# Two-layer hybrid decoder trunk in fp32: output tiles from both PSUM pools, one more pair by seven products, softmax division on either engine

## The chip, the cores and the metric

The kernel runs on one core of a Trainium2 chip. The metric is the device time of one execution in microseconds (us); the kernel before has a median of 2092.57 us over three runs (2092.12 to 2093.74). Engines are named as in the profile: PE (TensorE, matmul), DVE (VectorE), ACT (ScalarE), POOL (GpSimd), SP (SyncE, which issues the loads).

## The reference, cut to what matters

x is 512 tokens by 1024, c one row of 1024, everything fp32. Each of two layers does three sub-layers, each with a shift, a scale and a gate computed from c (adaLN). D_FF is 2816.

```python
for each layer:
    (shift, scale, gate) x 3 = SiLU(c) @ w_mod + b_mod
    x += 1/2 * gate1 * FFN1(RMSNorm(x) * scale1 + shift1)      # SwiGLU
    x += gate2 * (concat[A, B, C](RMSNorm(x) * scale2 + shift2, w_in) @ w_out)
    x += 1/2 * gate3 * FFN2(RMSNorm(x) * scale3 + shift3)
FFN(h) = (silu(h @ w_gate) * (h @ w_up)) @ w_down
A = stick-breaking attention (4 heads), B = dilated attention (4 heads, softmax over three
window patterns), C = HGRN2 gated linear recurrence (4 heads)
```

## The kernel before

**Numbers.** Activations lie transposed: 128 rows of the model dimension by 512 tokens, eight such tiles for x (`X[d]`). A product in fp32 is made of three matmuls on operands split into a high and a low part (`triple`). A weight tile is loaded as `w` (128x1024), cast to a high part by ACT (`wt<-w`) and subtracted to a low part by DVE (`wt<-w,wt`).

**Phases.** Net 0 (FFN1 of layer 0, to about 393 us), mixer 0 (to 698), net 1 (FFN2, to 1063), net 2 (FFN1 of layer 1, to 1418), mixer 1 (to 1723), net 3 (FFN2, to the end). `MOD` holds the adaLN columns; `background()` computes them for later sub-layers beside the nets: DVE accumulates rows of w_mod times c in `acc`, reduces `acc` to `p`, PE multiplies `p` by `quads` in one small matmul, and DVE writes four pieces of `mod`.

**One net (`ffn`).** The 22 hidden blocks of 128 go in three groups of 8, 8 and 6. In a group PE first makes the hidden blocks in pairs, gate then up, and then the eight output tiles of 128x512 (`x += gate * sum over the group's blocks`). A pair is dense (48 matmuls of 512 columns into pool `m` for the gate, 48 into pool `a` for the up) or, if its first block f is in `FAST[net]`, made by a scheme of seven products (`seven`, `empty`, `combine`): 84 matmuls of 256 columns for the gate and 84 for the up, with more sums of weights and partial results on DVE and ACT.

**PSUM.** Eight banks of 128x512 lie in two pools: `M` has two (named m in the profile), `B` has six (named a). A dense gate and, before, every output tile of a net take m banks; a gate by seven products takes two m and one a; an up takes two or three a. The small adaLN matmul and the sum of squares of the norm take an a bank.

**Output tiles.** The first two of a group are made by `down_two`, both at once, in two pieces (all blocks but the last two, then those). The others are made one by one by `down`. In the last group of nets 0 to 2 the last six are made in two halves of 256 columns. After each, `residual` on DVE adds the tile to x (`x<-m,mod,x`), which needs that sub-layer's `mod` and frees the bank.

**The head of a phase.** `first()` makes the first pair of the next phase for half of the tokens at a time; it asks for two m banks, then two a banks.

**What sets the order.** The program is static. At build time `Flow.run` keeps a list of streams, each at a `Step` on some engine, with estimated clocks of the engines (`F.clk`, `Flow.cost`) and estimated ready times of the tiles. It emits the step whose estimated start plus a bias is smallest, if the pools it needs have room. Every instruction is issued through `Engine.call`, so the profile has line L116 for nearly all. For a PE step of the background stream (rank 4) `Flow.start` adds `LATE` to the ready times of what it reads, so that it is put later in PE's order.

**Mixers.** Projections, and for each head tasks that run in four lanes beside them. `dilated` makes the softmax of the dilated heads: scores on PE, mask and maximum on DVE, exponential with its sum on ACT, reciprocal of the sum and division on DVE.

Of the kernel before, what the change touches and what calls it, by code (L numbers as in the profile page):

```python
# [14 lines left out]
AF = mybir.ActivationFunctionType  # L15
ALU = mybir.AluOpType
# [28 lines left out]


GROUPS = (8, 8, 6)
FAST = ((4, 8, 12, 16, 18), (4, 8, 10, 12, 14, 16, 18), (4, 8, 10, 12, 14, 16, 18), (4, 8, 10, 12, 14, 16, 18, 20))


PROJ = "f0,q0,g0,i0,qa,ka,va,q1,f1,g1,qb,i1,kb,vb"
# [11 lines left out]
BR = -0.15  # L63
BA = (-0.1, -0.1)
BN = (-0.15, -0.1)
LATE = 2.0
LOP = ((1, 2, 3), (1, 2, 3, 4, 5, 6, 7))

SPANS = tuple((sum(GROUPS[:i]), n) for i, n in enumerate(GROUPS))
# [159 lines left out]
class Flow:  # L229
# [96 lines left out]
    def start(self, s):  # L326
# [6 lines left out]
        t = self.clk[st.engine] if st.engine != "SP" else self.clk["PE"]  # L333
        late = self.MARGIN if st.engine == "PE" and s[0] == 0 else LATE if st.engine == "PE" and s[0] == 4 else 0.0
        for a in st.deps:
# [24 lines left out]
def trunk(ctx, tc, x, c, w_mod, b_mod, f1g, f1u, f1d, w_in, w_out, qng, kng, hng, lbl, f2g, f2u, f2d, cf, out):  # L360
    nc = tc.nc
    F = Flow()
    V, A, G, T, Q, Q2 = (Engine(F, e, n) for e, n in (
        (nc.vector, "DVE"), (nc.scalar, "ACT"), (nc.gpsimd, "POOL"), (nc.tensor, "PE"), (nc.sync, "SP"),
        (nc.gpsimd, "SP")))

    def space(name, bufs, **kw):
        return ctx.enter_context(tc.tile_pool(name=name, bufs=bufs, **kw))
# [8 lines left out]
    M = Pool(F, space("psm", 2, space=PS), "m", [P, S], 2)  # L377
    B = Pool(F, space("psa", 6, space=PS), "a", [P, S], 6)

    def small(w=1):  # L380
        return col.tile([P, 8], F32, tag="c", name="c")[:, :w]
# [33 lines left out]
    def when(*keys):  # L415
        return lambda: all(k in done for k in keys)
# [339 lines left out]
    def plan():  # L756
# [6 lines left out]
        for l in range(DEPTH):  # L763
            for wg, wu, wd, last in ((f1g, f1u, f1d, 0), (f2g, f2u, f2d, 1)):
                net = 2 * l + last
                its = []
                for f0, n in SPANS:
                    for f in range(f0, f0 + n, 2):
                        kind = "f" if f in FAST[net] else "w"
                        its += [(kind, [(0, w[l, :, f * P:(f + 2) * P], ND, 256)]) for w in (wg, wu)]  # L770
# [172 lines left out]
    def part(w, k, i=None):  # L943

        o = slice(0, 256) if i is None else slice(i * P, (i + 1) * P)
        return tuple(z[:, k % 4, o] for z in w[k // 4])

    def triple(ps, wh, wl, xh, xl, start, stop, skip=False):
        T.matmul(ps, wh, xh, start=start, stop=False, skip_group_check=skip)
        T.matmul(ps, wh, xl, start=False, stop=False, skip_group_check=skip)  # L950
        T.matmul(ps, wl, xh, start=False, stop=stop, skip_group_check=skip)
# [164 lines left out]
    def start_norm(phase, l, jsh, orders=(tuple(range(ND)),) * 2, after=None):  # L1116
        hs = [None] * ND
        hold.append(phase)
        quads4 = None if jsh == 3 or not FAST[2 * l + (jsh > 0)] else [[None] * 4 for _ in range(4)]
        for t in range(2):  # L1120
# [15 lines left out]
    def residual(phase, d, ps, l, jg, cs):  # L1136
        if jg != 5 or not isinstance(phase, tuple):
            yield when(("mod", l, jg))
        yield Step("DVE", ps, bias=BR)
        V.scalar_tensor_tensor(X[d][:, cs], ps[:, cs], mod(l, jg, d), X[d][:, cs], ALU.mult, ALU.add)  # L1140
        drop(ps)
        for t in range(2):
            if cs.start <= t * HALF and cs.stop >= (t + 1) * HALF:
                done.add((phase, d, t))
# [32 lines left out]
    def ffn(phase, l, jsh, hs, last):  # L1177
        jg = jsh + 2
        nhs = None
        fast = FAST[2 * l + (jsh > 0)]  # L1180
        for f0, n in SPANS:
# [58 lines left out]
            for f in range(f0, f0 + n, 2):  # L1240
# [15 lines left out]
                if f in fast:  # L1256
                    yield when((phase, "sums"))
                    for name, pools, fin in (("g", (M, M, B), gate_seven), ("u", (B, B, B), up_seven)):
                        w = yield from next_weight()
                        yield Step("PE", need=tuple((p, pools.count(p)) for p in (M, B) if p in pools))  # L1260
                        banks = [p.get() for p in pools]
# [6 lines left out]
                for pool, fin in ((M, gate_out), (B, up_out)):  # L1268
                    w = yield from next_weight()
                    for i in range(2):  # L1270
                        yield Step("PE", need=((pool, 1),))
                        ps = pool.get()
# [17 lines left out]

            def down(w, d, cs):
                yield when(keys[0])
                yield Step("PE", need=((M, 1),))
                ps = M.get()
                for k in range(n):
                    yield when(keys[k])
                    hi, lo = hid[k]
                    wh, wl = part(w, k, d % 2)
                    yield Step("PE", lo, wh, wl)
                    triple(ps[:, cs], wh, wl, hi[:, cs], lo[:, cs], k == 0, k == n - 1)  # L1300
                F.spawn(residual(key, d, ps, l, jg, cs), 0)

            def down_two(w, cuts):

                yield Step("PE", need=((M, 2),))
                banks = [M.get() for _ in range(2)]
                for ks in cuts:
                    for d, ps in enumerate(banks):
                        for k in ks:
                            yield when(keys[k])  # L1310
                            hi, lo = hid[k]
                            wh, wl = part(w, k, d)
                            yield Step("PE", lo, wh, wl)
                            triple(ps, wh, wl, hi, lo, k == 0, k == n - 1)
                        if ks[-1] == n - 1:
                            F.spawn(residual(key, d, ps, l, jg, FULL), 0)
# [4 lines left out]
            for d in range(0, whole, 2):  # L1321
                w = yield from next_weight()
                if d == 0:
                    yield from down_two(w, (range(n - 2), range(n - 2, n)))
                else:
                    for i in range(2):
                        yield from down(w, d + i, FULL)
                release(w)
# [32 lines left out]
    def mixer(phase, l, hs):  # L1361
# [4 lines left out]
        def key(*k):  # L1366
            return (phase, *k)
# [327 lines left out]
        def drop_qk(name, hp):  # L1695
            got["qk", name, hp] = got.get(("qk", name, hp), 0) + 1
            if got["qk", name, hp] == 2:
                U.put(*got["q" + name, hp], *got["k" + name, hp])
# [105 lines left out]
        def dilated(h):  # L1804
            hp, r = h // 2, 64 * (h % 2)
            yield when(key("qb", hp), key("kb", hp), *(key("vb", t) for t in range(NT)))
            qh, ql = got["qb", hp]
            kt = got["kb", hp][h % 2]
            kh, kl = kt[:, :S], kt[:, S:]
            yield Step("PE", ql, kt, need=((U, 9),))  # L1810
            sm = [U.get() for _ in range(3)]
            part = {3: sm[0], 2: sm[1][:, :384], 0: sm[1][:, 384:], 1: sm[2][:, :256]}
            for i in (3, 2, 1, 0):
                n = (i + 1) * P
                qc = slice(i * P, n)
                yield Step("PE", need=((B, 1),))
                s = B.get()
                T.matmul(s[:, :n], qh[:, qc], kh[:, :n], start=True, stop=False)
                T.matmul(s[:, :n], qh[:, qc], kl[:, :n], start=False, stop=False)
                T.matmul(s[:, :n], ql[:, qc], kh[:, :n], start=False, stop=True)  # L1820
                mx, den = small(), small()
                yield Step("DVE", s)
                V.tensor_tensor_reduce(part[i], s[:, :n], C["dil"][:, S - n:], 1.0, NEG, ALU.add, ALU.max, accum_out=mx)
                B.put(s)
                V.tensor_scalar(mx, mx, -1.0, None, ALU.mult)
                yield Step("ACT", mx)
                A.activation(part[i], part[i], AF.Exp, bias=mx, accum_out=den)
                yield Step("DVE", den)
                V.reciprocal(den, den)
                V.tensor_scalar(part[i], part[i], den, None, ALU.mult)  # L1830
            drop_qk("b", hp)
            wh, wl = [None] * 3, [None] * 3
            for b, cs in ((1, (1, 3)), (2, (2,)), (0, (0,))):
                n = WIDTH[b]
                yield Step("PE", *sm, need=((B, 1),))
                pt = B.get()
                for c_ in cs:
                    o = SEG[c_][1]
                    for i in range(c_, NT):
                        T.transpose(pt[:, o + (i - c_) * P:o + (i - c_ + 1) * P], part[i][:, c_ * P:(c_ + 1) * P], ident)  # L1840
                yield Step("ACT", pt, need=((U, 2),))
                wh[b], wl[b] = U.get(F32R), U.get(F32R)
                A.copy(wh[b][:, :n], pt[:, :n])
                yield Step("DVE", wh[b])
                V.tensor_sub(wl[b][:, :n], pt[:, :n], wh[b][:, :n])
                B.put(pt)
            U.put(*sm)
            yield from attend("b", "vb", h, wh, wl)
# [56 lines left out]
        for d in range(0, ND - 2, 2):  # L1905
            w = yield from next_weight()
            yield Step("PE", need=((M, 2),))
            banks = [M.get() for _ in range(2)]
# [10 lines left out]
        for t, cs in enumerate(HALVES):  # L1919
            for n, d in enumerate(order[t]):  # L1920
                pool = (M, B)[n % 2]
                yield Step("PE", need=((pool, 1),))
                ps = pool.get()
# [65 lines left out]
```

## Time and profile before

| | |
|---|---|
| median of three runs | 2092.57 us |
| the profiled execution | 2094.81 us, span 2092.4 us |
| mean granted TensorE clock | 0.992 |
| matmuls of 512 columns into m, into a | 3444, 800 |
| matmuls of 256 columns into m, into a | 3684, 3718 |
| weights and constants read | 255 MB, 123 GB/s over the span |

The costliest groups of instructions (engine, operation, tiles, forms, count, then busy us and mean ns of one, then idle time before them and its most frequent releaser):

```profile
L116 ACT CAST wt<-w 128x1024 fp32r<-128x1024 f32 (+1 forms) x456 | 437.6, 975 | 328.4 <-PE m L116 124.0
L116 DVE TENSOR_TENSOR wt<-w,wt 128x1024 fp32r<-128x1024 f32 (+1 forms) x456 | 518.6, 1144 | 95.3 <-ACT wt L116 86.2
L116 PE MATMUL m<-u,wt 128*128 128x512 f32 (+1 forms) x2820 | 576.7, 362 | 6.3 <-DVE x L116 4.2
L116 PE MATMUL m<-h,wt 128*128 128x256 f32 (+1 forms) x2892 | 551.8, 342 | 11.6 <-ACT h L116 5.5
```

A time in a group is the sum over its instructions; matmuls overlap one another, so the mean of one is longer than the distance from one to the next. A name such as m<-u,wt says that a tile of pool m was written from u and wt: m<-u,wt in a net is an output tile, m<-h,wt or a<-h,wt a dense gate or up, a<-hs,wt and m<-hs,wt belong to the seven products, and a<-p,quads is the small matmul of the adaLN columns. Rows of the timeline give the start, the length, the engine, the operation and its count; in brackets stands the idle time of the engine ahead of it and what ended it.

### The profile page before, as it was taken

The numbers are of one execution on the slowest core, as the hardware profiler recorded it, in microseconds if no ns is written. First come the engines' busy times: TensorE is split into PE (matmuls) and PEld (weight loads), VectorE is DVE, ScalarE is ACT, GpSimd is POOL, SyncE is SP. The second block draws the span as 40 slices with busy tenths as digits, with TensorE's granted clock in tenths as the row PEclk, the third lists the DMA queues.
The fourth block names the chain that finished last, engine by engine and source line by source line (L and its number), as shares of the span: only waits on it lengthen the run. The fifth ranks groups of instructions, "written<-read, shape, count | busy, mean of one in ns | idle before, by whom it ended". The sixth has DMA issues, their size and how long they took to land.

```text
span 2092.4 us, 32600 instructions
## 1 busy us (share of the span) xinstructions
PE 2050.3 (98%) x12956; PEld 1855.7 (89%) x12956; DVE 1586.0 (76%) x2510; ACT 1005.1 (48%) x1675; POOL 183.6 (9%) x224
## 2 busy tenths in 40 slices
PE   7999999999999999999999999999999999999999
PEld 6888889988888987999898899989888889889897
DVE  6887877686698776879686888867867978658584
ACT  5523434555855542544354253436476645325351
POOL 0000000150150100000010000012304200000000
PEclk8999999999999999999999999999999999999999
DMA  9376466211203245345524635643112141533321
GB/s 330 117 230 191 151 218 204 81 60 41 71 21 99 94 133 169 109 154 182 181 69 134 221 101 181 197 146 102 41 41 66 36 127 55 186 96 101 101 82 41
DMA packets 210569, 259.46 MB, mean 124 GB/s; under 512 B 8896, under 2 KB 192084, under 8 KB 210416
## 3 DMA queue, kind: packets, MB, share of 16 engines
q1 hardware_dynamic: 210160, 257.30, 38.5%
q8 instruction: 101, 1.65, 0.3%
q14 instruction: 52, 0.43, 0.1%
q0 software_dynamic: 256, 0.08, 0.0%
HBM read 255.25 MB, written 2.10 MB: 123 GB/s over the span
## 4 chain that ended last, share of the span: by engine, by line
PE 93%; DVE 4%; ACT 2%; issue 1%; DMA 1%; SPq 0%; DVEq 0%; ACTq 0%
PE m L116 56%; PE a L116 37%; ACT u L116 1%; DVE u L116 1%; DVE wt L116 1%; DVE x L116 1%; DVE h L116 1%; DVE acc L116 0%; ACT wt L116 0%; DMA w<-in_ffn_w_up_dram 0%; DMA u<-in_x_dram 0%; DVE k L116 0%; ACT L1471 0%; ACT L116 0%; SPq L116 0%
## 5 line engine op out<-in xcount | busy, mean ns | idle before, releaser
L116 ACT CAST wt<-w 128x1024 fp32r<-128x1024 f32 (+1 forms) x456 | 437.6, 975 | 328.4 <-PE m L116 124.0
L116 DVE TENSOR_TENSOR wt<-w,wt 128x1024 fp32r<-128x1024 f32 (+1 forms) x456 | 518.6, 1144 | 95.3 <-ACT wt L116 86.2
L116 PE MATMUL m<-u,wt 128*128 128x512 f32 (+1 forms) x2820 | 576.7, 362 | 6.3 <-DVE x L116 4.2
L116 PE MATMUL m<-h,wt 128*128 128x256 f32 (+1 forms) x2892 | 551.8, 342 | 11.6 <-ACT h L116 5.5
L116 PEld LDWEIGHTS m<-u,wt 128*128 128x128 f32 x2820 | 475.4, 190 | 85.7 <-DVE x L116 5.6
L116 PEld LDWEIGHTS m<-h,wt 128*128 128x128 f32 x2892 | 451.0, 192 | 69.4 <-ACT u L116 6.6
L116 PE MATMUL a<-h,wt 128*128 128x256 f32 (+1 forms) x2124 | 347.4, 318 | 0.0
L116 PEld LDWEIGHTS a<-h,wt 128*128 128x128 f32 x2124 | 308.3, 191 | 26.5
L116 DVE TENSOR_TENSOR u<-u 128x256 f32<-128x256 f32 (+4 forms) x444 | 255.3, 593 | 34.5 <-ACT u L116 30.7
L116 PE MATMUL a<-hs,wt 128*128 128x256 f32 x1944 | 250.8, 283 | 0.0
L116 POOL TENSOR_TENSOR u<-u 128x256 f32<-128x256 f32 x162 | 137.6, 869 | 1284.8 <-ACT u L116 1237.5
L116 PEld LDWEIGHTS a<-hs,wt 128*128 128x128 f32 x1944 | 241.0, 192 | 0.0
L116 DVE SCALAR_TENSOR_TENSOR x<-m,mod,x 128x512 f32<-128x512 f32 (+1 forms) x142 | 92.2, 651 | 111.7 <-PE m L116 111.0
L116 ACT ACTIVATE u<-u 128x512 f32<-128x512 f32 (+2 forms) x272 | 146.7, 567 | 49.2 <-POOL u L116 29.3
L116 DVE TENSOR_TENSOR w<-w 128x512 f32<-128x512 f32 x216 | 149.0, 690 | 6.2 <-DMA w<-in_ffn_w_gate_dram 0.6
L116 DVE SCALAR_TENSOR_TENSOR acc<-w,sc_c,acc 128x1024 f32<-128x1024 f32 x112 | 143.6, 1282 | 1.8
L116 PEld LDWEIGHTS a<-u 128*128 128x128 f32 x864 | 114.7, 191 | 11.8 <-issue 2.1
L116 ACT COPY u<-a 128x256 f32<-128x256 f32 (+1 forms) x149 | 58.1, 390 | 129.9 <-PE a L116 127.6
L116 PE MATMUL a<-u 128*128 128x64 f32 (+4 forms) x864 | 117.0, 282 | 1.9 <-DVE u L116 0.8
L116 ACT COPY u<-m 128x256 f32<-128x256 f32 (+1 forms) x119 | 49.7, 418 | 123.4 <-PE m L116 117.2
L116 ACT CAST u<-u 128x512 fp32r<-128x512 f32 (+1 forms) x96 | 58.4, 611 | 102.7 <-DVE u L116 93.4
L116 PE MATMUL m<-wt,h 128*128 128x256 f32 x768 | 99.7, 287 | 0.9 <-DVE u L116 0.9
(146 smaller groups left out, 1452.6 us busy)
## 6 DMA issues: line engine op xcount, KB each, us to landing
w<-in_w_mod_dram SPq DMA_DIRECT2D x128, 512.0 KB, 4.3
w<-in_ffn_w_gate_dram SPq DMA_DIRECT2D x88, 512.0 KB, 4.7
w<-in_ffn_w_up_dram SPq DMA_DIRECT2D x88, 512.0 KB, 4.9
w<-in_ffn_w_down_dram SPq DMA_DIRECT2D x80, 512.0 KB, 4.7
w<-in_w_in_dram SPq DMA_DIRECT2D x56, 512.0 KB, 3.8
u<-in_w_mod_dram SPq DMA_DIRECT2D x32, 256.0 KB, 6.0
w<-in_w_out_dram SPq DMA_DIRECT2D x24, 256.0 KB, 3.1
w<-in_ffn_w_down_dram SPq DMA_DIRECT2D x16, 256.0 KB, 5.7
```

What stands on the lines that cost most here:

```text
L116: ins = fn(*args, **kw)
```

## The change

Four edits. The list of pairs by seven products for net 1 (the second tuple) gets f=20, its last pair. `LATE` goes from 2.0 to 4.0. Output tiles of a net take their bank from `M` and `B` in turn: an even d from `M`, an odd d from `B`; `down_two` takes one of each. In `dilated` the division by the sum goes to ACT as a copy with a scale where the planner's clock of ACT is more than 0.5 us behind that of DVE at that point, and stays on DVE otherwise.

```diff
-FAST = ((4, 8, 12, 16, 18), (4, 8, 10, 12, 14, 16, 18), (4, 8, 10, 12, 14, 16, 18), (4, 8, 10, 12, 14, 16, 18, 20))
+FAST = ((4, 8, 12, 16, 18), (4, 8, 10, 12, 14, 16, 18, 20), (4, 8, 10, 12, 14, 16, 18), (4, 8, 10, 12, 14, 16, 18, 20))
...
-LATE = 2.0
+LATE = 4.0
...
             def down(w, d, cs):
                 yield when(keys[0])
-                yield Step("PE", need=((M, 1),))
-                ps = M.get()
+                pool = (M, B)[d % 2]
+                yield Step("PE", need=((pool, 1),))
+                ps = pool.get()
...
             def down_two(w, cuts):
 
-                yield Step("PE", need=((M, 2),))
-                banks = [M.get() for _ in range(2)]
+                yield Step("PE", need=((M, 1), (B, 1)))
+                banks = [M.get(), B.get()]
...
                 V.reciprocal(den, den)
-                V.tensor_scalar(part[i], part[i], den, None, ALU.mult)
+                if F.clk["ACT"] + 0.5 < F.clk["DVE"]:
+                    A.activation(part[i], part[i], AF.Copy, scale=den)
+                else:
+                    V.tensor_scalar(part[i], part[i], den, None, ALU.mult)
```

Over the whole program PE has 96 matmuls of 512 columns fewer and 168 of 256 more. Of the 512-column ones 2502 now write m and 1646 write a (before 3444 and 800). Four of the 32 divisions go to ACT, all four 512 columns wide.

PE's order where the first group of net 1 ends and its output tiles begin (in the trace of before at 768 to 838 us), before the change:

```order
L116 MATMUL m<-h,wt 128x512 x48
L116 MATMUL a<-h,wt 128x512 x48
L116 MATMUL m<-u,wt 128x512 x42
L116 MATMUL a<-p,quads 128x32
L116 MATMUL m<-u,wt 128x512 x150
L116 MATMUL m<-h,wt 128x256 x12
```

And with the change:

```order
L116 MATMUL m<-h,wt 128x512 x48
L116 MATMUL a<-h,wt 128x512 x48
L116 MATMUL m<-u,wt 128x512 x18
L116 MATMUL a<-u,wt 128x512 x18
L116 MATMUL m<-u,wt 128x512 x6
L116 MATMUL a<-u,wt 128x512 x6
L116 MATMUL m<-u,wt 128x512 x3
L116 MATMUL a<-p,quads 128x32
L116 MATMUL m<-u,wt 128x512 x21
L116 MATMUL a<-u,wt 128x512 x24
L116 MATMUL m<-u,wt 128x512 x24
```

The small matmul moved from behind 42 output matmuls to behind 51 (18 + 18 + 6 + 6 + 3), and the output tiles alternate between m and a.

DVE's order at the same place (wt is a weight split, u a hidden block, x_84 to x_86 tiles of x, mod_92 the adaLN columns of layer 0), before:

```order
L116 TENSOR_TENSOR wt<-w,wt 128x1024
L116 TENSOR_TENSOR u<-u 128x512
L116 SCALAR_TENSOR_TENSOR acc<-w,sc_c,acc 128x1024 x2
L116 TENSOR_REDUCE p<-acc 128x32
L116 SCALAR_TENSOR_TENSOR mod_92<-a,bcol_94 32x8 x4
L116 SCALAR_TENSOR_TENSOR x_84<-m,mod_92,x_84 128x512
L116 TENSOR_TENSOR wt<-w,wt 128x1024
L116 SCALAR_TENSOR_TENSOR x_85<-m,mod_92,x_85 128x512
```

And with the change:

```order
L116 TENSOR_TENSOR wt<-w,wt 128x1024
L116 TENSOR_TENSOR u<-u 128x512
L116 SCALAR_TENSOR_TENSOR acc<-w,sc_c,acc 128x1024 x2
L116 TENSOR_REDUCE p<-acc 128x32
L116 TENSOR_TENSOR wt<-w,wt 128x1024 x2
L116 SCALAR_TENSOR_TENSOR mod_92<-a,bcol_94 32x8 x4
L116 SCALAR_TENSOR_TENSOR x_84<-m,mod_92,x_84 128x512
L116 SCALAR_TENSOR_TENSOR x_85<-a,mod_92,x_85 128x512
```

Up to p nothing moved; two weight splits went ahead of the writes of mod and of the first addition, and the second addition now reads an a bank.

ACT's order in mixer 0 (at 482 to 488 us in the trace of before) around the second pair of casts for k, the keys of the stick-breaking heads, which lie in an m bank until DVE has subtracted the cast part. The rows with eps_c and behind it are logarithm and exponential of an HGRN head's norm. Before:

```order
L116 COPY u<-a 128x512
L116 ACTIVATE u<-a 128x512
L116 CAST k<-m 64x512 x2
L116 CAST wt<-w 128x1024
L116 ACTIVATE u<-a,eps_c 128x512
L116 ACTIVATE u<-u 128x512
```

And with the change:

```order
L116 COPY u<-a 128x512
L116 ACTIVATE u<-a 128x512
L116 CAST wt<-w 128x1024
L116 CAST k<-m 64x512 x2
L116 ACTIVATE u<-a,eps_c 128x512
L116 ACTIVATE u<-u 128x512
```

The cast of a weight tile moved ahead of the casts for k. On DVE the row ahead of k by which the norm is applied (u<-u,par) belonged before to a norm that ACT had done earlier; with the change it belongs to the norm whose two activations stand behind the casts for k, here the last two rows:

```order
L116 TENSOR_TENSOR wt<-w,wt 128x1024
L116 COPY u<-a 128x128
L116 SCALAR_TENSOR_TENSOR u<-u,a 128x128 x2
L116 TENSOR_TENSOR u<-u 128x512
L116 SCALAR_TENSOR_TENSOR u<-u,par 128x512
L116 TENSOR_TENSOR u<-u 128x512
L116 TENSOR_TENSOR k<-m,k 64x512 x2
```

These are DVE's rows up to the second subtraction for k, with the change; it stands behind the two u operations.

## The prediction

> **What bounds the kernel now.** First the page's line of busy times, then its chain that ended last:
>
> ```profile
> span 2092.4 us, 32600 instructions
> PE 2050.3 (98%) x12956; PEld 1855.7 (89%) x12956; DVE 1586.0 (76%) x2510; ACT 1005.1 (48%) x1675; POOL 183.6 (9%) x224
> PE 93%; DVE 4%; ACT 2%; issue 1%; DMA 1%; SPq 0%; DVEq 0%; ACTq 0%
> ```
>
> The reader is to see that TensorE (PE) is busy for all but 42.1 us of the span. VectorE (DVE) is idle for a quarter of it and ScalarE (ACT) for half. So only three things change the time: columns that PE no longer multiplies, waits of PE that go or come, and stretches in which PE runs at a lower clock. Work on DVE or ACT counts only where PE waits behind it. The second view is therefore the waits of PE by releaser (columns: us in total, times, longest).
>
> ```profile
> PE m L116 <- DVE x L116: 7.5, 10, 2.0
> PE a L116 <- ACT u L116: 6.3, 10, 1.2
> PE m L116 <- ACT h L116: 5.5, 6, 1.7
> PE m L116 <- ACT u L116: 4.9, 6, 1.7
> PE a L116 <- DVE p L116: 2.8, 1, 2.8
> ```
>
> The first and last rows are what the change can reach. In the first, PE waits with an output tile in an "m" bank until DVE has added an older tile to x: only two m banks exist. The last is one wait of the adaLN product for p. The two add to 10.3 us, 0.5% of the span. Differences under 0.2% (about 4.2 us) count as no change below, since a measurement of this kernel can hardly tell less.
>
> **Two pools and LATE at net 1.** The timeline around 800 us:
>
> ```profile
> 790.47 9.68 PE L116 MATMUL m<-u,wt 128*128 128x512 f32 x42
> 799.05 2.60 DVE L116 SCALAR_TENSOR_TENSOR acc<-w,sc_c,acc 128x1024 f32<-128x1024 f32 x2
> 801.68 1.25 DVE L116 TRANSPOSE_TENSOR_REDUCE p<-acc 128x32 f32<-128x1024 f32 x1
> 802.98 0.64 PE L116 MATMUL a<-p,quads 128*128 128x32 f32 x2 [2.83 <-DVE p L116]
> ```
>
> PE's 42 matmuls end at 800.15, and it stands 2.83 us until p is reduced. DVE's rows up to p are the same after the change. The small matmul now stands behind 51 output matmuls instead of 42. One costs 9.68/42 = 0.23 us (a little of this is the last one's tail; 0.227 by the pair of 48 in 10.91 us quoted below), so PE arrives 9 × 0.227 = 2.04 us later, with useful work. 0.8 us of waiting is left. Term: **−2.0**.
>
> What follows such a wait costs more. Granted clock (columns: window, length, PE busy (count), clock, DMA share, GB/s):
>
> ```profile
> 802.10:808.93 6.83, 5.95 (x15) 0.50 0.58 194
> 808.93:815.76 6.83, 6.83 (x31) 1.00 0.27 77
> 1829.51:1832.92 3.41, 3.41 (x9) 0.50 1.10 347
> 1832.92:1836.34 3.42, 3.42 (x16) 1.00 0.53 171
> ```
>
> Within 6.83 us after the wait the clock was half: 15 matmuls against 31. Taking out the 0.88 us that belongs to the wait itself, 5.95 us did the work of some 15 × 0.22 = 3.3 us, so 2.6 us were lost. At 1829 it is 9 against 16 in 3.41 us: 7 × 0.22 = 1.5 us. Waits of 1.7 us and less in the list above were followed by full clock, those of 2.83 and 2.04 by half. With 0.8 us left at 802 I take the stretch as gone: **−2.6**. Its bounds are 0 and −2.6. By the Trainium skill ("TensorE: Matmul & The Clock Gate", Part 1: The HAM clock gate) half rate comes after a whole idle window of about 3.4 us. This trace disagrees, since 2.83 and 2.04 us sufficed; by that rule neither stretch would be due to these waits, and neither would go. The page also calls the window free-running, so that an equal wait may trigger it in one execution and not in another.
>
> **Two pools at net 2 and net 3.**
>
> ```profile
> 1160.13 2.60 DVE L116 SCALAR_TENSOR_TENSOR acc<-w,sc_c,acc 128x1024 f32<-128x1024 f32 x2
> 1162.64 0.75 DVE L116 SCALAR_TENSOR_TENSOR x<-m,mod,x 128x512 f32<-128x512 f32 x1
> 1163.44 5.07 PE L116 MATMUL m<-u,wt 128*128 128x512 f32 x21 [1.50 <-DVE x L116]
> 1826.00 0.69 DVE L116 SCALAR_TENSOR_TENSOR mod<-a,bcol 32x8 f32<-32x8 f32 x4 [1.71 <-PE a L116]
> 1826.72 1.23 DVE L116 TENSOR_TENSOR wt<-w,wt 128x1024 fp32r<-128x1024 f32 x1
> 1827.98 1.41 DVE L116 SCALAR_TENSOR_TENSOR x<-m,mod,x 128x512 f32<-128x512 f32 x2
> 1828.79 12.58 PE L116 MATMUL m<-u,wt 128*128 128x512 f32 x47 [2.04 <-DVE x L116]
> ```
>
> In net 2 both m banks hold finished tiles; DVE adds the first only after two products acc (2.60 us). With down_two in one m and one a bank, the third tile finds a free m bank and the fourth a free a bank, so the addition has 24 matmuls (5.4 us) longer. The wait of 1.50 us and the 0.16 us that its restart adds to matmul spacing go: **−1.7**. In net 3 the addition comes behind the writes of mod and a weight split; the rows of DVE are nearly as before, but PE no longer needs that bank. 2.04 + 0.17 and the 1.5 us of half clock go: **−3.7** (bounds −2.2 and −3.7). No next wait is near: the adaLN column is ready when x is first due, and later additions take 0.75 us against a tile's 5.4.
>
> **Two pools at the head of the next phase.** The first pair of a phase needs both m banks, just after the last output tile, which held one.
>
> ```profile
> 394.71 2.78 PE L116 MATMUL m<-h,wt 128*128 128x256 f32 x21 [0.50 <-DVE x L116]
> 1063.98 2.77 PE L116 MATMUL m<-h,wt 128*128 128x256 f32 x21 [0.50 <-DVE x L116]
> 1419.66 2.53 PE L116 MATMUL m<-h,wt 128*128 128x256 f32 x19 [0.50 <-DVE x L116]
> ```
>
> The last output tile (the odd one) now sits in an a bank, so these three go: 3 × 0.66 with the restart, **−2.0**. The wait for h some 1 us ahead of each stays.
>
> **Net 1, f=20 by seven products.** The dense pair is 96 matmuls of 512 columns; seven products are 168 of 256. From the chain (start, length):
>
> ```profile
> 326.84 10.08 PE a L116 x84
> 726.91 10.91 PE m L116 x48
> 737.82 10.88 PE a L116 x48
> 968.11:988.27 20.16, 20.16 (x171) 20.16 (x170) 17.54 (x27) 11.73 (x20) 0.00 (x0) 1.00 0.52 172
> ```
>
> 10.91 + 10.88 = 21.79 against 2 × 10.08 = 20.16: **−1.6**. The last row is a stretch of seven products in net 1 (PE, PEld, DVE, ACT, POOL busy): DVE is busy 17.54 of 20.16 us, PE all of it, so the extra combining and weight sums hide behind PE as they do there. If DVE were the bound at the net's end instead, the term would be near +1: the next thing needed there is the split hidden tiles. I keep −1.6; bounds −1.6 and +1.
>
> **The division on ACT.** Four of 32 divisions move, all 512 wide. No row of PE's waits names a division; on the path it costs nothing, and its cover is the projections beside which the dilated lanes run. But the change shifts the order of the mixers otherwise. In mixer 0 (and likewise in mixer 1) the second pair of k tiles frees its m bank later:
>
> ```profile
> 485.12 1.05 ACT L116 CAST wt<-w 128x1024 fp32r<-128x1024 f32 x1
> 485.13 1.39 DVE L116 TENSOR_TENSOR k<-m,k 64x512 fp32r<-64x512 f32 x2 [1.06 <-ACT k L116]
> 486.19 0.69 ACT L116 ACTIVATE u<-a,eps_c 128x512 f32<-128x512 f32 x1
> 486.91 0.63 ACT L116 ACTIVATE u<-u 128x512 f32<-128x512 f32 x1
> 487.70 0.74 DVE L116 SCALAR_TENSOR_TENSOR u<-u,par 128x512 f32<-128x512 f32 x1
> 488.48 0.69 DVE L116 TENSOR_TENSOR u<-u 128x512 f32<-128x512 f32 x1
> ```
>
> Before, DVE subtracts k as soon as ACT has cast it. Now ACT casts a weight tile first (1.05 us), and DVE's subtraction stands behind the product with par and the u operation that wait for ACT's two activations behind the casts: 1.05 + 0.69 + 0.63 + 0.74 + 0.69 = 3.8 us later. One tile of tokens, 24 matmuls of 256 columns, goes into the other bank meanwhile: 24 × 0.12 = 2.9 us. I estimate that the remaining 0.9 us reaches PE in each mixer, and that small waits at each output projection shrink by 0.4. Together **+1.0**; bounds 0 and +3 (covered by other work, or 1.5 in each mixer because the chain begins later too).
>
> **Loads that come later.** Output tiles in a banks and a seventh block change which buffer a load waits for. In net 0's third group the order puts the load of one up weight behind a buffer that PE reads late. A transfer then takes
>
> ```profile
> w<-in_ffn_w_up_dram SPq DMA_DIRECT2D x88, 512.0 KB, 4.9
> ```
>
> 4.9 us, and the seven products may wait on ACT like the ten waits above (0.63 us on average, 1.2 at most). I take **+1.0**; bounds 0 and +1.6. LATE alone moves only these small adaLN matmuls; at other places they stand behind matmuls enough that PE waited for none, and stay at nothing.
>
> **The sum.** −2.0 − 2.6 − 1.7 − 3.7 − 2.0 − 1.6 + 1.0 + 1.0 = −11.6. The profiled execution took 2094.81 us (span 2092.4 and 2.4 around it), so 2083.2; the median of the runs, 2092.57, is 2.24 lower, so **2081.0**. With each unknown term at its one or its other bound the sum lies between −13.6 and −2.3: 2079.0 to 2090.3.
>
> **The rivals.**
> 1. *The clock stretches stay.* A wait of 0.8 us remains at 802, and another may form at the same places. Against it: waits of 1.7 us left full clock. Without the −2.6 and −1.5 the time is 2081.0 + 4.1 = 2085. The Trainium skill's rule (Part 1 of the page named above) would give this same result.
> 2. *The waits only move.* At 12 group ends PE must meet something else that is late: hidden tiles, weight casts, the first seven-product. About 1.0 us at each (as the mean 0.63 to 1.2 of the ACT u row) eats 11.6: no change, 2092. For it: DVE and ACT do the same work in the same time, and PE gets to each place sooner. Against it: the added time goes to places where DVE is idle, with 24% idle in all. Also, if only the moved divisions mattered, no bank being scarce, it would come out here.
> 3. *Slower: a banks run out.* The output tiles now take from the six a banks, which the next group's first block of seven needs at once: one a bank for its gate and three for its up. If the additions that free them are late, PE waits where it did not. The price is an addition behind two acc products, 2.60 + 0.75 = 3.4 us at most, at the 8 group ends followed by more blocks; it decides from 11.6/8 = 1.45 us each. At 2.2 us each: 8 × 2.2 − 11.6 = +6, so 2098. Against it: the output tiles hold at most two of the six a banks at a time, the gate needs one, and its 10.08 us pass before the up needs three.
>
> **How the numbers follow.** The forecast 0.66, rival 1 0.18, rival 2 0.10, rival 3 0.06. The forecast's own range is 2078 to 2085: the sum's lower bound and 1 us for the spread of runs, and at the other end half of the unknown terms. The whole, with rival 1 and part of rival 2, and leaving out no more than 2 in 10, is 2078 to 2089. Faster by over 0.2% means below 2088.4: the forecast, rival 1 and a little of rival 2, 0.85; within 0.2%: 0.09; slower 0.06.
>
> **What would show it.** Right: no half clock in the records near 802 and 1829; the row "m from DVE x" down from 7.5 us to under 2; the wait for p under 1 us; 168 matmuls of 256 where net 1 had the last dense pair; no new row "a from DVE x" above 1 us. Wrong: PE's busy time falls by less than 1.6 + 4 us while its waits stay; a half-clock stretch in another place; the second k subtraction of a mixer followed by over 1.5 us of waiting; net 1's end with PE waiting on DVE or ACT u.

## The result and the profile after

| | median of the runs | ratio to before, 95% interval |
|---|---|---|
| before | 2092.94 us (4 runs) | |
| with the change | 2081.51 us (2080.87 to 2082.53, 4 runs) | 0.9950 (0.9937 to 0.9962) |
| with the change, again | 2082.17 us (5 runs; before beside it: 2091.42) | 0.9961 (0.9949 to 0.9973) |

The change makes the kernel 9 to 11 us faster, 0.4 to 0.5%. The page of the changed kernel, the lines that answer to those of before:

```profile
span 2079.3 us, 32768 instructions
PE 2041.1 (98%) x13028; PEld 1852.5 (89%) x13028; DVE 1594.7 (77%) x2523; ACT 1013.5 (49%) x1694; POOL 190.9 (9%) x224
PE 92%; DMA 2%; DVE 2%; ACT 2%; issue 1%; POOL 0%; SPq 0%; POOLq 0%; DVEq 0%; ACTq 0%
```

PE is still busy 98% of the span, and 9.2 us shorter; the other 3.9 us of the 13.1 were idle time of PE. Its waits now (us in total, times, longest):

```profile
PE a L116 <- ACT u L116: 6.5, 10, 1.2
PE m L116 <- ACT h L116: 4.9, 3, 1.7
PE m L116 <- ACT u L116: 4.4, 6, 1.7
...
PE m L116 <- DVE x L116: 1.8, 2, 0.9
...
PE a L116 <- POOL u L116: 0.9, 1, 0.9
...
PE a L116 <- DVE p L116: 0.8, 1, 0.8
```

The row of m banks behind x fell from 7.5 us in ten waits to 1.8 in two; these two stand behind the mixers, whose output tiles the change leaves alone. The wait for p fell from 2.8 to 0.8. A wait for POOL (0.9) is new in this profile; a second profile of the changed kernel does not have it. By stage, cut at the first matmul of mixer 0, net 1, net 2, mixer 1, net 3 and the last transposition (columns: window, length, PE busy (count), granted clock, DMA share, GB/s), before:

```profile
393.60:700.50 306.90, 300.02 (x1934) 1.00 0.22 70
700.50:1062.90 362.40, 358.09 (x2305) 0.99 0.45 143
1062.90:1418.60 355.70, 353.53 (x2305) 1.00 0.47 151
1418.60:1725.50 306.90, 300.05 (x1934) 1.00 0.22 70
1725.50:2088.10 362.60, 356.72 (x2292) 0.99 0.31 95
```

And with the change:

```profile
392.10:699.10 307.00, 300.26 (x1936) 1.00 0.23 73
699.10:1055.90 356.80, 354.87 (x2375) 0.99 0.43 139
1055.90:1409.30 353.40, 353.20 (x2309) 1.00 0.48 155
1409.30:1716.50 307.20, 300.33 (x1937) 1.00 0.23 73
1716.50:2075.00 358.50, 353.69 (x2291) 1.00 0.31 97
```

Net 1 gave 5.6 us, net 2 2.3, net 3 4.1; the mixers gave nothing. Net 0 is 1.5 us shorter in this execution, but not by the change: the opening, which it does not touch, ended 2.1 us earlier (the matmul behind its last wait, for ACT u, starts at 85.28 us before and at 83.15 now; in the second profile of the changed kernel at 84.19). The three places in nets 1 to 3, in the timeline of PE with the change:

```profile
801.07 0.84 PE L116 MATMUL m<-u,wt 128*128 128x512 f32 x3
802.70 0.41 PE L116 MATMUL a<-p,quads 128*128 128x32 f32 x2 [0.79 <-DVE p L116]
802.94 5.03 PE L116 MATMUL m<-u,wt 128*128 128x512 f32 x21
...
1154.88 5.60 PE L116 MATMUL m<-u,wt 128*128 128x512 f32 x24
1160.32 5.60 PE L116 MATMUL a<-u,wt 128*128 128x512 f32 x24
...
1818.63 0.31 PE L116 MATMUL a<-p,quads 128*128 128x32 f32 x2
1818.78 4.34 PE L116 MATMUL m<-u,wt 128*128 128x512 f32 x18
```

At 802 0.79 us of the 2.83 are left. In nets 2 and 3 the output tiles follow one another without a bracket: no wait.

### The profile page after: what moved, and what is told of

The parts are those of the page before. It is cut to its first block, busy times and chain, and to the rows that moved or that the text cites. A ratio compares the mean times of both kernels' runs of the same rounds, so it can differ in the third digit from the quotient of the medians.

```text
span 2079.3 us, 32768 instructions
## 1 busy us (share of the span) xinstructions
PE 2041.1 (98%) x13028; PEld 1852.5 (89%) x13028; DVE 1594.7 (77%) x2523; ACT 1013.5 (49%) x1694; POOL 190.9 (9%) x224
## 4 chain that ended last, share of the span: by engine, by line
PE 92%; DMA 2%; DVE 2%; ACT 2%; issue 1%; POOL 0%; SPq 0%; POOLq 0%; DVEq 0%; ACTq 0%
PE a L116 47%; PE m L116 45%; DMA u<-in_w_mod_dram 1%; ACT u L116 1%; DMA w<-in_ffn_w_up_dram 1%; DVE u L116 1%; ACT wt L116 1%; DVE wt L116 0%; DVE acc L116 0%; POOL u L116 0%; DMA u<-in_x_dram 0%; SPq L116 0%; DVE x L116 0%; DVE w L116 0%; DVE k L116 0%
## 5 line engine op out<-in xcount | busy, mean ns | idle before, releaser
L116 PE MATMUL m<-h,wt 128*128 128x256 f32 (+1 forms) x2880 | 543.1, 340 | 9.9 <-ACT h L116 4.9
L116 PE MATMUL m<-u,wt 128*128 128x512 f32 (+1 forms) x1602 | 336.6, 359 | 2.9 <-DVE wt L116 1.5
L116 PE MATMUL a<-h,wt 128*128 128x256 f32 (+1 forms) x2112 | 338.7, 315 | 0.0
L116 PEld LDWEIGHTS m<-u,wt 128*128 128x128 f32 x1602 | 267.2, 189 | 45.0 <-DVE wt L116 1.9
L116 PE MATMUL a<-u,wt 128*128 128x512 f32 (+1 forms) x1386 | 279.1, 353 | 0.0
L116 PEld LDWEIGHTS a<-u,wt 128*128 128x128 f32 x1386 | 229.4, 189 | 34.6
L116 PE MATMUL a<-hs,wt 128*128 128x256 f32 x2016 | 260.1, 283 | 0.0
L116 PEld LDWEIGHTS a<-hs,wt 128*128 128x128 f32 x2016 | 250.0, 192 | 0.0
L116 ACT COPY u<-a 128x256 f32<-128x256 f32 (+2 forms) x154 | 59.9, 389 | 122.9 <-PE a L116 120.2
L116 DVE SCALAR_TENSOR_TENSOR x<-m,mod,x 128x512 f32<-128x512 f32 (+1 forms) x85 | 54.5, 641 | 77.9 <-PE m L116 77.6
```

The lines of the kernel that those rows point to most:

```text
L116: ins = fn(*args, **kw)
```

## The experiments

Each was timed in five to eleven runs beside the kernel before, whose medians were 2091.4 to 2092.1 us.

**Each edit alone.** Four kernels, each the kernel before with one of the four hunks. First the output tiles in both pools:

```diff
-                yield Step("PE", need=((M, 1),))
-                ps = M.get()
+                pool = (M, B)[d % 2]
+                yield Step("PE", need=((pool, 1),))
+                ps = pool.get()
...
-                yield Step("PE", need=((M, 2),))
-                banks = [M.get() for _ in range(2)]
+                yield Step("PE", need=((M, 1), (B, 1)))
+                banks = [M.get(), B.get()]
```

> The kernel before with one edit, the output tiles of the nets from both pools. My theory (bank waits): the waits of PE for x in net 2 (1.5 us), in net 3 (2.0) and at the heads of three phases (0.5 each) go, and the half-clock stretch at the start of net 3's output tiles with them: 1.7 + 3.7 + 2.0 = 7.4 us less, about 2085.5; the small adaLN matmul of net 1 still stands behind 42 output matmuls, so its wait of 2.8 us and the 6.8 us at half clock stay. Rival (the freed waits only move): 2092 to 2093, with new waits of PE at the next tiles. Rival (a banks run out): slower, with rows 'a from DVE x' of over 1 us.

Measured: 2083.42 us, ratio 0.9957 (0.9944 to 0.9969), 8.7 us less. The waits in nets 2 and 3 and at the three heads are gone; the wait for p stands:

```profile
799.99 0.41 PE L116 MATMUL a<-p,quads 128*128 128x32 f32 x2 [2.83 <-DVE p L116]
```

But in this profile no half clock followed it (below). This edit carries most of the gain.

```diff
-LATE = 2.0
+LATE = 4.0
```

> The kernel before with one edit, LATE 4.0. The small adaLN matmul of net 1 stands behind 48 output matmuls (before 42), that of net 3 behind 48 (before 45). My theory: the wait for p falls from 2.8 to about 1.5 us; if the half clock comes from the length of the wait and 1.5 us is too short for it, 2.6 us more go: about 2089; if not, 2091.5. In net 3 mod is written later, while PE still waits for that m bank: up to 0.7 us more there, so 2089 to 2092. Rival (LATE is what carries the whole gain): 2083 or less.

Measured: 2096.27 us, ratio 1.0022 (1.0011 to 1.0034): slower by 4.2 us, which neither theory gave. The timeline at net 1's first output tiles:

```profile
804.22 0.41 PE L116 MATMUL a<-p,quads 128*128 128x32 f32 x2 [1.47 <-DVE p L116]
...
806.32 0.68 DVE L116 SCALAR_TENSOR_TENSOR mod<-a,bcol 32x8 f32<-32x8 f32 x4
807.04 1.41 DVE L116 SCALAR_TENSOR_TENSOR x<-m,mod,x 128x512 f32<-128x512 f32 x2
807.84 2.50 PE L116 MATMUL m<-u,wt 128*128 128x512 f32 x5 [3.22 <-DVE x L116]
```

The wait for p halved as expected. But the small matmul now stands behind all 48 matmuls of the first two tiles, both m banks are full, and the next tile needs one of them. That bank is freed by the addition to x, which needs mod, which needs the small matmul. So PE waits a second time, 3.2 us, while DVE splits two weight tiles, writes mod and adds: 4.7 us for 2.8. With one pool, putting the matmul later only lengthens the chain that holds the bank.

That chain is less than half of the loss: net 1 is 1.7 us longer. LATE also moved the order elsewhere. In net 0 stands a wait that the kernel before does not have:

```profile
299.35 1.69 PE L116 MATMUL m<-hs,wt 128*128 128x256 f32 x12 [1.66 <-ACT u L116]
```

And both mixers are 1.1 us longer, from the first matmul of the mixer to that of the next net (306.92 to 308.05 and 306.96 to 308.02 us), with a new wait of 0.18 us for k in each. In net 3 the wait for the m bank shrank, from 2.04 to 1.57 us.

```diff
-FAST = (..., (4, 8, 10, 12, 14, 16, 18), ...)
+FAST = (..., (4, 8, 10, 12, 14, 16, 18, 20), ...)
```

> The kernel before with one edit, the last pair of net 1 by seven products. My theory: 96 matmuls of 512 columns at 0.227 us become 168 of 256 at 0.120 us, 1.6 us less: about 2091.3, with no new wait over 0.5 us in net 1. Rival (DVE becomes the bound at net 1's end): PE waits for u there and the time is 2093 to 2095.

Measured: 2088.28 us, ratio 0.9983 (0.9974 to 0.9991): 1.9 to 5.4 us less. The 1.6 from the columns and a wait that is gone with them (0.4 us for ACT u in the pair before, at 994 us in the trace of before; 0.5 with its restart) make 2.1. The wait of 1.50 us for the m bank in net 2 is gone too, although the tiles lie in m banks only: in this order DVE has added the first tile at 1157.75 us, before PE comes to the third at 1158.26. That is 1.7 more. Against it stands a new wait of 0.25 us for ACT u at 1114 us, 0.4 with its restart. Together 3.4, where the medians differ by 3.8. So the edits overlap: the pools and this edit each take away the wait in net 2. No new wait came in net 1.

```diff
-                V.tensor_scalar(part[i], part[i], den, None, ALU.mult)
+                if F.clk["ACT"] + 0.5 < F.clk["DVE"]:
+                    A.activation(part[i], part[i], AF.Copy, scale=den)
+                else:
+                    V.tensor_scalar(part[i], part[i], den, None, ALU.mult)
```

> The kernel before with one edit, the division on either engine. Four of the 32 divisions go to ACT. My theory: no change, 2092.9 within 1 us, since PE waited for none of them; waits in the mixers shift by some tenths. Rival (the order that this edit gives the mixers carries part of the gain): 2 us or more less, with fewer waits of PE in the mixers.

Measured: 2092.03 us, ratio 1.0003 (0.9995 to 1.0012): no change. The wait for POOL of 0.9 us after mixer 1 appears here too, and in none of the three other kernels with one edit. But the changed kernel has it in one profile of two, so this edit alone does not decide it.

**LATE back to 2.0 in the changed kernel.** Alone LATE costs 4.2 us; do the edits add up?

> The changed kernel with LATE back at 2.0. Net 1's small adaLN matmul stands behind 42 output matmuls again. My theory (LATE costs PE only through the wait for the m bank behind mod, which two pools take away, so together they pay): the wait for p is 2.8 us again (2.0 more) and may bring up to 2.6 us of half clock; the waits of 0.9 us near 297 us and of some 0.5 us at the head of each mixer go: 2081.5 to 2084.5, not faster than the changed kernel. Rival (the edits add up, and LATE costs the 4.2 us that it costs alone): 2077 to 2079.6.

Measured: 2083.92 us, ratio 0.9963 (0.9949 to 0.9976). It is not faster than the changed kernel, so the costs do not add: the second pool takes away the second wait in net 1 that LATE costs alone. The wait near 297 us is gone, as expected, and so are those for k: they come with LATE in the changed kernel too. Whether LATE gains 1.8 us there is not settled, since the intervals overlap.

**The other edits with one pool.** The changed kernel with the two hunks on pools undone.

> The changed kernel with its output tiles in m banks only, as before: LATE 4.0, the seventh pair and the division stay. My theory (LATE without the second pool costs what it cost alone): 2091.8 + 4.2 - 3.8 = 2092 within 1.5 us, with net 1 waiting for p (1.5 us) and then for the addition to x in an m bank (3.2 us), and the waits of 0.5 us for x at the heads of the phases back. Rival (the second pool only hides half of it, the order of the rest carries the gain): 2085 to 2088.

Measured: 2092.13 us, ratio 1.0006 (0.9998 to 1.0015), where my theory gave 2092. The same two waits as with LATE alone are back (1.47 and 3.22 us). The one in net 2 is not, as with the seven products alone. In the company of the other edits the second pool is worth 10 us (2092.13 against 2082.17).

**LATE 5.0 in the changed kernel.**

> The changed kernel with LATE 5.0. The small matmul of net 1 stands behind 57 output matmuls, so its wait for p (0.8 us) goes. My theory: that saves 0.8 us there, but in net 2 the order of DVE and ACT brings the weights of the dense pair near 1100 us later, and PE waits there some 8 to 10 us: 2088 to 2092. Rival (later is better): 2080.5.

Measured: 2089.74 us, ratio 0.9995 (0.9987 to 1.0004). The wait for p is gone, but net 2 waits for weights. PE, then ACT at the same place:

```profile
1084.98 1.22 PE L116 MATMUL m<-h,wt 128*128 128x512 f32 x2 [8.78 <-ACT wt L116]
1088.41 2.07 PE L116 MATMUL m<-h,wt 128*128 128x512 f32 x4 [2.21 <-DVE wt L116]
```
```profile
1083.36 0.62 ACT L116 CAST hs<-u 128x512 fp32r<-128x512 f32 x1 [1.49 <-DVE u L116]
1083.88 5.35 ACT L116 CAST wt<-w 128x1024 fp32r<-128x1024 f32 x6
```

The planner put six casts of weights behind a row of casts for hs, each of which waits for DVE. Why a later small matmul brings that order was not traced.

**All divisions on DVE in the changed kernel.**

> The changed kernel with all 32 divisions on DVE. My theory: no change within 1 us, 2080.5 to 2082.5; the wait for POOL of 0.9 us near 1723 goes, the waits at the output projections of the mixers (0.7 + 0.4 + 1.0) become those of before (0.3 + 0.4 + 0.8 + 0.6). Rival (in the changed order the moved divisions carry some of the gain): 2 us or more slower than the changed kernel.

Measured: 2080.68 us, ratio 0.9953 (0.9940 to 0.9965): the same as the change within the intervals. The wait for POOL is gone, as expected, but the second profile of the changed kernel lacks it too.

**Every output tile of the nets in an a bank.** This tests the rival of a shortage of a banks.

```diff
-                pool = (M, B)[d % 2]
+                pool = B
...
-                yield Step("PE", need=((M, 1), (B, 1)))
-                banks = [M.get(), B.get()]
+                yield Step("PE", need=((B, 2),))
+                banks = [B.get(), B.get()]
```

> The changed kernel with every output tile of the nets in an a bank, none in an m bank: it asks for more a banks than the change does. My theory (a banks are not scarce there): the same as the changed kernel within 1.5 us, 2080 to 2083, no row 'a from DVE x' over 1 us beside the last one at the end. Rival (the change runs close to a shortage of a banks): 2085 to 2095, with waits of PE for x in a banks at the group ends.

Measured: 2082.03 us, ratio 0.9955 (0.9942 to 0.9967), and the row "a from DVE x" is the one at the end alone (0.8 us), as before the change. Six banks are enough even for twice the demand.

**The mixers' last tiles.** Both waits for x that are left stand where a net begins behind a mixer. By the same rule as in the nets, the second half of the mixer's last tiles goes to a banks (divisions on DVE):

```diff
-                pool = (M, B)[n % 2]
+                pool = (M, B)[n % 2] if t == 0 else B
```

> The changed kernel with all divisions on DVE and the tiles of the second half of each mixer's last output projection all in a banks, so that the next net's first pair finds both m banks free. My theory: the waits for x of 0.9 us at 699 and 1717 us go, 1.0 each; the wait for h of 1.6 us ahead of them stays: 2080.7 - 2.0 = 2078.7, and less where the half clock behind them goes. Rival (the h tiles are as late as x, so that the wait only changes its name): 2080.7.

Measured: 2082.72 us, ratio 0.9967 (0.9955 to 0.9979): not the 2 us that I expected, and no less than the changed kernel beside it (2082.17). The timeline of PE with the change, and in this run:

```profile
699.14 0.59 PE L116 MATMUL m<-h,wt 128*128 128x256 f32 x3 [1.61 <-ACT h L116]
700.62 6.63 PE L116 MATMUL m<-h,wt 128*128 128x256 f32 x31 [0.89 <-DVE x L116]
```
```profile
700.42 0.98 PE L116 MATMUL m<-h,wt 128*128 128x256 f32 x6 [0.60 <-DVE h L116]
702.82 0.98 PE L116 MATMUL m<-h,wt 128*128 128x256 f32 x6 [1.42 <-DVE h L116]
704.10 1.42 PE L116 MATMUL m<-h,wt 128*128 128x256 f32 x5 [0.30 <-DVE h L116]
```

The wait only changed its name: the tiles of h are late as well, since the norm of the same x makes them. Here the rival was right. In the nets the bank was late alone; here bank and data come from one chain.

**And LATE 3.75.** The run with the mixers' tail in a banks, with LATE 3.75.

> As the run with the mixers' tail in a banks, with LATE 3.75. Net 1's small matmul stays behind 51 output matmuls (wait for p 0.8 us); my theory: the wait of 0.8 us near 297 us in net 0 goes, nothing else changes: 1 us less than that run, 2077.7 where that one is at 2078.7. Rival: no difference, because the load that is late there comes from the order of the pools and not from LATE.

Measured: 2091.91 us, ratio 1.0004 (0.9996 to 1.0013), which neither theory gave. The wait near 297 us stays (0.6 us). In both mixers, at 486 and 1507 us, a new one stands:

```profile
488.73 1.58 PE L116 MATMUL m<-wt,h 128*128 128x256 f32 x8 [2.85 <-DVE k L116]
```

That is the wait that the prediction priced at 0.9 us for the changed kernel, in an order in which it is 2.85 us; in this profile half clock followed both. A quarter of a microsecond in LATE moves the planner's order in places that have nothing to do with it.

**The changed kernel again.**

> The changed kernel again, beside the others on one chip: 2081.5 within 1 us. In its profile I look at whether the same waits are followed by half clock as in the first one; if the clock depended on the waits alone, the same stretches would be at half clock (696 us, not 802 and not 1717).

Measured: 2082.17 us. The waits from net 1 on are those of the first profile, without two of them (0.87 us for POOL at 1724 us, 0.21 for ACT u at 902); the one near 298 us is 0.93 us instead of 0.71. The stretches at half clock are not the same: here they follow the waits near 698, 1691 and 1715 us, there only the one near 696.

## Why the prediction was right

The forecast was 2081.0 us; 2081.51 and 2082.17 were measured. Its terms against the runs:

| term | predicted | measured |
|---|---|---|
| net 1, wait for p | −2.0 | 2.83 to 0.79: −2.0 |
| net 1, half clock behind it | −2.6 | gone in both profiles, but not tied to the wait alone |
| net 2, m bank | −1.7 | 1.50 to 0 (−1.7 with the restart) |
| net 3, m bank and half clock | −3.7 | wait gone (−2.2); the clock as above |
| three heads | −2.0 | −3.0: the wait for h went too |
| net 1, seven products | −1.6 | −2.1: a wait for ACT u went too (edit alone −1.9 to −5.4, with the wait in net 2) |
| mixers | +1.0 | about +1.6, and it comes with LATE |
| net 0, late load | +1.0 | 0.7 us of waiting at 298: +0.9, and it comes with LATE |

*The banks.* That the scarce thing was a second free m bank, not DVE's speed, is shown by the pools alone (−8.7 us) and by the tiles in a banks alone (the same time as the change). The a banks did not run out, and the waits did not move to the group ends: rivals 2 and 3 are out.

*The heads.* "The wait for h some 1 us ahead of each stays" was wrong: in the changed kernel the first pair begins with no wait at all. At 0.17 us each, 0.33 with the restart, that is 1.0 us more.

*The mixers.* The k banks cost less than I thought (waits of 0.17 us), but each mixer stage, which before held one of the head waits of 0.66 us, is as long as before: 0.1 and 0.2 us longer (306.92 to 307.01 and 306.96 to 307.17 us) with 0.66 less in it, so +0.75 and +0.87. The waits at the output projections did not shrink by 0.4 each: they are 1.40 and 1.25 us before, 1.44 and 1.45 now. The prediction put the shifted order of k under the division. The runs put it under LATE: alone it makes both stages 1.1 us longer and brings the waits for k, while with the pools alone the stages are 306.09 and 306.12 us, shorter by the head wait. Where in the mixer the part beyond the waits lies was not traced. The new wait for POOL (0.9) came on top in net 3, in the first profile.

*LATE.* The prediction put the whole of net 1's wait down to "Two pools and LATE" and did not price LATE alone. It is no gain by itself: 4.2 us slower. "LATE alone moves only these small adaLN matmuls; at other places they stand behind matmuls enough" overlooked that mod, x and the bank hang on such a matmul. It was wrong on the order too: the wait in net 0 and the late k tiles, which the prediction put down to the pools, the seventh block and the shifts beside the division, are there with LATE alone and with none of the other three edits alone.

*The clock.* The two half-clock terms (−4.1 together) were taken as the price of those waits. That price is not paid each time. The same wait of 2.83 us at net 1 was followed by half clock before and by full clock with the pools alone; the wait of 2.04 us at net 3 by half clock before and by full clock with the division alone. The reading "Waits of 1.7 us and less in the list above were followed by full clock" does not hold in the trace of before. Behind mixer 1 its waits of 1.61 us for h and 0.89 us for x fall into one window, and the next is at half clock (columns as above):

```profile
1723.70:1727.11 3.41, 0.91 (x6) 1.00 0.66 191
1727.11:1730.52 3.41, 3.41 (x16) 0.50 0.34 117
```

The same happens behind mixer 0, near 703 us. The change leaves these waits in place, and half clock followed them near 700 us in both profiles and near 1718 in one. Over the runs on record the mean granted clock is 0.9939 before (61 runs) and 0.9943 with the change (9 runs). From this difference of 0.0004 in 2090 us I estimate that the clock gave about 1 us, not 4.1. So rival 1 was not a case of its own but a share of every execution; the last section shows on what it hangs.

*The sum.* Without the clock the prediction's terms add up to −7.5 and the measured ones to −8.5, or −7.6 with the wait for POOL. With 1 us from the clock that makes 8.6 to 9.5, where the medians differ by 9.3 in the second comparison and by 11.4 in the first. The banks carry the gain as forecast. That the number came within 0.5 us of the first median is in part luck: the clock term was some 3 us too large, the other terms together 1 us too small, and the kernel before was slower in that comparison (2092.94) than beside the experiments (2091.4 to 2092.1).

## What to carry to other kernels

Where PE is the bound, look for the wait that holds a bank: a second pool of banks took 9 us from waits that DVE, at 76%, did not explain. Before an instruction is put later on the engine that waits for it, ask what hangs on its result, and whether that holds the resource which the next instruction needs: LATE made net 1 1.7 us longer with one pool, and with two it took 2 us off the wait there. A planner's parameter also acts far from the place it is meant for: LATE made net 0 and both mixers longer as well. And freeing a bank pays only where the data do not come from the same chain.

## What the runs showed of the hardware

In the traces, stretches of half clock last whole multiples of 3.41 us (3.41 and 6.83 in most places, 10.24 at the start; the last is cut by the end) and begin on a fixed grid of that period in each execution. How much of a wait falls into one window of the grid counts, not its length alone. The windows around net 1's wait of 2.83 us, before, and with the pools alone:

```profile
795.28:798.69 3.41, 3.41 (x17) 1.00 0.00 0
798.69:802.10 3.41, 1.47 (x7) 1.00 0.73 227
802.10:805.51 3.41, 2.53 (x7) 0.50 0.97 324
```
```profile
795.08:798.49 3.41, 2.08 (x10) 1.00 0.48 151
798.49:801.90 3.41, 1.91 (x9) 1.00 1.08 359
801.90:805.31 3.41, 3.41 (x16) 1.00 0.32 105
```

Before, most of the wait lies in one window (PE busy 1.47 us of 3.41), and the next runs at half clock. With the pools alone the grid's edge cuts the wait in two (2.08 and 1.91 us busy), and the clock stays. The wait of 2.04 us at net 3, before, and with the division alone:

```profile
1826.10:1829.51 3.41, 1.37 (x6) 1.00 1.10 357
1829.51:1832.92 3.41, 3.41 (x9) 0.50 1.10 347
```
```profile
1829.38:1832.79 3.41, 1.71 (x9) 1.00 1.07 365
1832.79:1836.20 3.41, 3.06 (x13) 1.00 1.10 350
```

1.37 us busy brought half clock, 1.71 did not. The limit is not sharp in these numbers: behind the opening, windows with 1.47 us or less were all followed by half clock, but so were some with 1.61 to 2.06, nearly all of them in the mixers or at the head of the net behind one. What besides the busy time counts is open. The Trainium skill ("TensorE: Matmul & The Clock Gate", Part 1: The HAM clock gate) states that half rate comes after at least one whole idle window; in these traces less than a whole idle window was enough. Its free-running window agrees with the grid. Where the grid falls differs from execution to execution. That goes with the spread of the runs: of 61 runs of the kernel before beside the experiments, the 32 with a mean clock of 0.993 took 2092.8 us on average, the 18 with 0.995 or more 2089.5. A difference of 2 us between two kernels can be this alone.
